# A Winograd convolution on one core: five edits to how it loads, warms up and stores

## The chip, the cores and the metric

The kernel runs on one core of a Trainium2 chip. Its time is in device microseconds (us); the lower the better. A set of runs is told by its median. The profile is of one execution, taken by the hardware profiler; its times are from the start of the span.

## The reference

A 3x3 convolution with padding 1 over 16 images of 64 channels and 64 x 64 pixels, to 128 output channels, all float32:

```python
def setup_inputs():
    batch, c_in, h, w, c_out = 16, 64, 64, 64, 128
    return {
        "x": np.random.randn(batch, c_in, h, w).astype(np.float32),
        "weight": np.random.randn(c_out, c_in, 3, 3).astype(np.float32) * 0.1,
    }

def reference(x, weight):
    x_pad = np.pad(x, ((0, 0), (0, 0), (1, 1), (1, 1)), mode='constant')
    ...
                        output[b, co] += weight[co, ci, kh, kw] * x_pad[b, ci, kh:kh+h, kw:kw+w]
    return output
```

The input is 16.8 MB and the output 33.6 MB.

## The kernel before, in words

Two images make a pair: 2 x 64 input channels fill the 128 partitions, so there are 8 pairs (`NP`), and each pair is worked on in two halves of 16 row pairs. `for n, (p, h) in enumerate(halves)` runs over the 16 halves. In the vertical direction the kernel computes two output rows at once (a Winograd scheme): from the input rows it forms sums (`ss`, L111), differences (`dd`, L118) and outer differences (`ee`, L124) in 16-bit floats, and a 16-bit copy of 17 rows (`xh`, L129). The first half's transforms are VectorE's (DVE), the second half's and all later ones are GpSimd's (POOL), which works two halves ahead; `xh` is ScalarE's (ACT), one half ahead. The seven weight combinations `Wt` (G0, G1, G2, G21, G01, HP, HM) are made once at the start: POOL casts the raw weights to `w16` (L82), TensorE (PE) transposes them by a multiplication with the identity (L98, in two runs, so that the result stands in partitions 0 to 63 and in 64 to 127), ACT and DVE combine them (L136 to L147).

`mms` (L167) issues the matmuls of a half, 54 of them, for the two images of the pair in turn (contraction over 64 partitions each). `copies` (L189, ACT) takes partial results out of PSUM, and DVE (L224, L226, L228) and ACT (L230) put together the output rows in `ots`, one tile of 128 output channels for each image. PSUM tiles with the tag "acc" share 8 buffers in turn; the first of them are used for the weights.

Inputs `xs` and outputs `ots` of 2.10 MB each share nine buffers of SBUF. Which one each uses is written out by hand: `X_HOME` for the loads, `O_HOME` for the two outputs of a pair. A tile's buffer is written again only when all that read it are done, a store's landing included.

Each engine works in the order in which the code names its instructions (`keep`). All transfers are issued by SyncE (SP), in one queue: the weights, the first pair in two pieces (rows 0 to 33, then 34 to 63), pairs 1 to 5; then, as results come, the stores, and the loads of pairs 6 and 7 behind the stores of pairs 2 and 3. Stores are of a whole image; only those of the last pair are cut by rows, 32 in each half. `spin` issues matmuls over a tile of zeros: 7 ahead of the weights' transposes and 9 behind them. Their result is not used.

Of the kernel before, what the change touches and what calls it, by code (L numbers as in the profile page):

```python
# [8 lines left out]
F32 = mybir.dt.float32  # L9
F16 = mybir.dt.float16  # L10
# [5 lines left out]
def kernel(  # L16
# [12 lines left out]
    nc = tc.nc  # L29
    B, CI, H, W = x.shape  # L30
    CO = weight.shape[0]
    assert H == 64 and W == 64 and CI == 64 and CO == 128 and B == 16
    NP = B // 2
    RB = 8

    keep = tc.keep_in_program_order
# [3 lines left out]
    const = ctx.enter_context(tc.tile_pool(name="const", bufs=1))  # L40
    psum = ctx.enter_context(tc.tile_pool(name="psum", bufs=8, space=bass.MemoryType.PSUM))
# [3 lines left out]
    upool = ctx.enter_context(tc.tile_pool(name="upool", bufs=8))  # L45

    X_HOME = [0, 1, 2, 3, 4, 7, 3, 4]
    O_HOME = [(6, 5), (8, 0), (1, 6), (2, 5), (8, 0), (1, 6), (7, 2), (5, 3)]

    def home(k, name):  # L50
        return slots.tile([128, H, W], F32, tag=f"s{k}", name=name)

    w_raw = const.tile([CO, CI * 9], F32)
# [3 lines left out]
    def load(p, cuts=((0, H),)):  # L57
        xs[p] = home(X_HOME[p], "xs")
        for lo, hi in cuts:
            keep(  # L60
                nc.sync.dma_start(
                    xs[p][:, lo:hi, :], x_rows[128 * p : 128 * p + 128, lo:hi, :]
                )
            )

    load(0, ((0, 34), (34, H)))
    for p in range(1, 6):
        load(p)

    zeros = const.tile([128, 512], F16)  # L70
    keep(nc.vector.memset(zeros, 0.0))  # L71
    warm = psum.tile([128, 512], F32, tag="acc", name="warm")

    def spin(n):
        for _ in range(n):
            keep(nc.tensor.matmul(warm, zeros[:, 0:128], zeros))  # L76

    spin(7)
    ident = const.tile([128, 128], F16)
    make_identity(nc, ident)  # L80
    w16 = const.tile([CO, CI * 9], F16)
    keep(nc.gpsimd.tensor_copy(w16, w_raw))  # L82

    G0, G1, G2, G21, G01, HP, HM = range(7)
    Wt = const.tile([128, 7, 3, CO], F16)
# [7 lines left out]
    for kh in (0, 2, 1):  # L93
        wp = psum.tile([128, 512], F32, tag="acc", name="wp")
        for k in range(3):
            t = 3 * kh + k
            for q in (0, 64):
                keep(nc.tensor.matmul(wp[q : q + 64, k * CO : k * CO + CO], w16[:, t::9], ident))  # L98
        wps[kh] = wp[:, 0 : 3 * CO]
    spin(9)  # L100


    F_BLK, G_BLK = (1, 2), (0, 3)
# [23 lines left out]
    def cast(p, h):  # L127
        t = cpool.tile([128, 17, W], F16, tag="xh", name="xh")
        keep(nc.scalar.copy(t, xs[p][:, C_ROW[h] : C_ROW[h] + 17, :]))  # L129
        return t  # L130

    def transforms(eng, p, h):
        return sums(eng, p, h), diffs(eng, p, h), outers(eng, p, h)
# [17 lines left out]
    def mms(tiles, terms, start, stop):  # L151
        n = 3 * len(terms)
        i = 0
        for wi, src, row in terms:
            for kw in (1, 0, 2):
                c_lo, c_hi = max(0, 1 - kw), min(W, W + 1 - kw)
                lo, hi = 0, RB
                at, step, rows = row
                while at + step * lo < 0:
                    lo += 1  # L160
                while at + step * (hi - 1) > rows - 1:
                    hi -= 1
                first, last = at + step * lo, at + step * (hi - 1)
                for b2 in range(2):
                    p0 = 64 * b2
                    keep(
                        nc.tensor.matmul(  # L167
                            tiles[b2][:, lo:hi, c_lo:c_hi],
                            Wt[p0 : p0 + 64, wi, kw, :],
                            src[  # L170
                                p0 : p0 + 64,
                                first : last + 1 : step,
                                c_lo + kw - 1 : c_hi + kw - 1,
                            ],
                            start=start and i == 0,
                            stop=stop and i == n - 1,
                            skip_group_check=not start,
                        )
                    )
                i += 1  # L180

    def acc():
        return [psum.tile([128, RB, W], F32, tag="acc", name="acc") for _ in range(2)]

    def copies(tiles):
        us = []
        for b2 in range(2):
            ut = upool.tile([128, RB, W], F32, tag="ut", name="ut")
            keep(nc.scalar.copy(ut, tiles[b2]))  # L189
            us.append(ut)  # L190
        return us

    halves = [(p, h) for p in range(NP) for h in range(2)]

    def store(eng, p, b2, ot, lo, hi):
        keep(eng.dma_start(out[2 * p + b2, :, lo:hi, :], ot[:, lo:hi, :]))  # L196

    for n, (p, h) in enumerate(halves):
        if n + 2 < len(halves):
            tr[halves[n + 2]] = transforms(nc.gpsimd, *halves[n + 2])  # L200
        if h == 0:
            ots = [home(k, "ot") for k in O_HOME[p]]
            ov = [t.rearrange("p (j i) c -> p j i c", i=2) for t in ots]
        ss, dd, ee = tr.pop((p, h))
        xc = xh.pop((p, h))
        jf, jg = RB * F_BLK[h], RB * G_BLK[h]
        sf, sg = jf - 16 * h, jg - 16 * h
        g_at = 2 * jg - C_ROW[h]

        pf1, pg1, pf2, pg2 = acc(), acc(), acc(), acc()  # L210
        mms(pf1, [(HP, ss, (sf, 1, 16))], True, True)
        ux = copies(pf1)
        mms(pg1, [(G1, ss, (sg, 1, 16))], True, True)
        ug = copies(pg1)
        mms(pf2, [(HM, dd, (0, 1, RB))], True, True)
        uy = copies(pf2)
        if n + 1 < len(halves):
            xh[halves[n + 1]] = cast(*halves[n + 1])
        mms(pg2, [(G01, xc, (g_at, 2, 17)), (G2, xc, (g_at + 2, 2, 17))], True, True)
        mms(pf1, [(G0, ee, (0, 2, 16))], False, True)  # L220
        mms(pg1, [(G21, xc, (g_at + 1, 2, 17)), (G0, xc, (g_at - 1, 2, 17))], False, True)
        mms(pf2, [(G2, ee, (1, 2, 16))], False, True)
        for b2 in range(2):
            keep(nc.vector.tensor_add(ov[b2][:, jg : jg + RB, 1, :], pg2[b2], ug[b2]))  # L224
        for b2 in range(2):
            keep(nc.vector.tensor_add(ov[b2][:, jf : jf + RB, 0, :], pf1[b2], uy[b2]))  # L226
        for b2 in range(2):
            keep(nc.vector.tensor_sub(ov[b2][:, jf : jf + RB, 1, :], ux[b2], pf2[b2]))  # L228
        for b2 in range(2):
            keep(nc.scalar.copy(ov[b2][:, jg : jg + RB, 0, :], pg1[b2]))  # L230
        if h == 1 or p == NP - 1:
            lo, hi = (0, H) if p < NP - 1 else (32 * h, 32 * h + 32)
            store(nc.sync, p, 0, ots[0], lo, hi)
            store(nc.sync, p, 1, ots[1], lo, hi)
            if p in (2, 3):
                load(p + 4)


# [28 lines left out]
```

## Time and profile before

| | |
|---|---|
| Median of 3 runs | 128.31 us (127.98 to 128.99) |
| The profiled execution | 127.76 us |
| Its span in the profile | 125.8 us |
| PE / PEld busy | 100.2 / 49.9 us |
| DVE / ACT / POOL busy | 67.3 / 84.8 / 90.5 us |
| The queue of all transfers | 50.63 MB, 95.8% of the span of 16 DMA engines |
| HBM read / written | 17.07 / 33.55 MB |
| Loads of 2.10 MB, from issue to landing | 20.3 us (median) |
| Stores of 2.10 MB, from issue to landing | 18.2 us (median) |

How to read it: PE is the matmuls, PEld the loading of their weights beside them. "L124" is a line of the kernel. The span is cut into 40 slices of equal length; a digit is the busy share of a slice in tenths. "A <- B" in a list of waits says that A waited and B ended the wait. The span does not hold all of the execution's time: 2.0 us lie around it.

### The profile page before, as it was taken

How to read it: one execution, taken by the hardware profiler on the slowest of the kernel's cores; microseconds unless marked ns; L12 is line 12 of the kernel's file. 1: busy time of each engine (PE TensorE's matmuls, PEld its weight loads, DVE VectorE, ACT ScalarE, POOL GpSimd, SP SyncE). 2: the span in 40 equal slices, each digit the busy share in tenths (PEclk: the TensorE clock that was granted, in tenths of full speed). 3: DMA queues.
4: the chain of work that ended last, by engine and by line, in shares of the span. 5: the costliest groups of instructions: out<-in, count | busy, mean ns of one | idle time of the engine just before them, and what ended most of it. 6: DMA issues, size and time to landing. Idle time of an engine off the chain costs nothing.

```text
span 125.8 us, 2404 instructions
## 1 busy us (share of the span) xinstructions
PE 100.2 (80%) x898; PEld 49.9 (40%) x898; DVE 67.3 (53%) x105; ACT 84.8 (67%) x149; POOL 90.5 (72%) x52
## 2 busy tenths in 40 slices
PE   6997899999993799999999999999999995000000
PEld 2443444444441355555555555555555552000000
DVE  0299849393820956749393947657493939000000
ACT  4269398979792679898979797898989783000000
POOL 2209999999999999999999999999999300000000
PEclk9999999999999999999999999999999999855555
DMA  5899999999999999999999999999999999999970
GB/s 144 351 438 438 427 433 433 422 422 417 360 425 427 427 425 443 427 417 420 433 433 433 422 433 417 433 433 435 422 427 427 422 453 412 433 412 425 422 313 18
DMA packets 4043, 50.78 MB, mean 404 GB/s; under 512 B 448, under 2 KB 448, under 8 KB 704
## 3 DMA queue, kind: packets, MB, share of 16 engines
q1 hardware_dynamic: 4032, 50.63, 95.8%
q8 instruction: 7, 0.11, 0.3%
q14 instruction: 4, 0.03, 0.1%
HBM read 17.07 MB, written 33.55 MB: 403 GB/s over the span
## 4 chain that ended last, share of the span: by engine, by line
PE 57%; DMA 19%; DVE 7%; DVEq 0%; ACT 0%; issue 0%; SPq 0%; ACTq 0%
PE acc L167 57%; DMA out_dram<-ot 15%; DMA xs<-in_x_dram 5%; DVE ee L124 2%; DVE ot L228 1%; DVE ot L226 1%; DVE ss L111 1%; DVE dd L118 0%; DVEq L262 0%; ACT ot L230 0%; DVE Wt L145 0%; DVE Wt L142 0%; DVE Wt L147 0%; SPq L54 0%; SPq L196 0%
## 5 line engine op out<-in xcount | busy, mean ns | idle before, releaser
L167 PEld LDWEIGHTS <-Wt 64*128 64x128 f16 x864 | 47.0, 94 | 50.3 <-issue 4.4
L189 ACT COPY ut<-acc 128x512 f32<-128x512 f32 x96 | 48.6, 612 | 4.4 <-PE acc L167 4.3
L167 PE MATMUL acc<-xh,Wt 64*128 64x504 f16 (+3 forms) x384 | 49.7, 370 | 0.0
L111 POOL TENSOR_TENSOR ss<-xs 128x1024 f16<-128x1024 f32 x15 | 35.6, 2373 | 5.3 <-DMA xs<-in_x_dram 5.3
L224 DVE TENSOR_TENSOR ot<-acc,ut 128x512 f32<-128x512 f32 x32 | 20.7, 686 | 33.2 <-ACT ut L189 19.6
L124 POOL TENSOR_TENSOR ee<-xs 128x1024 f16<-128x1024 f32 x15 | 35.6, 2372 | 0.0
L167 PE MATMUL acc<-ee,Wt 64*128 64x504 f16 (+1 forms) x192 | 30.3, 377 | 1.3 <-DVE ee L124 1.3
L167 PE MATMUL acc<-ss,Wt 64*128 64x504 f16 (+1 forms) x192 | 26.0, 377 | 2.9 <-DVE ot L224 2.6
L230 ACT COPY ot<-acc 128x512 f32<-128x512 f32 x32 | 17.3, 589 | 12.0 <-PE acc L167 10.1
L228 DVE TENSOR_TENSOR ot<-ut,acc 128x512 f32<-128x512 f32 x32 | 20.5, 683 | 0.6 <-PE acc L167 0.4
L226 DVE TENSOR_TENSOR ot<-acc,ut 128x512 f32<-128x512 f32 x32 | 20.4, 680 | 0.0
L118 POOL TENSOR_TENSOR dd<-xs 128x512 f16<-128x512 f32 x15 | 20.3, 1350 | 0.0
L129 ACT CAST xh<-xs 128x1088 f16<-128x1088 f32 x16 | 18.4, 1152 | 0.0
L167 PE MATMUL acc<-dd,Wt 64*128 64x504 f16 (+1 forms) x96 | 15.1, 377 | 0.0
L76 PE MATMUL warm<-zeros 128*128 128x512 f16 x16 | 5.8, 527 | 1.2 <-DVE zeros L71 1.2
L76 PEld LDWEIGHTS <-zeros 128*128 128x128 f16 x16 | 1.8, 124 | 3.9 <-issue 2.1
L138 DVE SCALAR_TENSOR_TENSOR th<-wp,g0h 128x384 f32<-128x384 f32 x1 | 0.6, 558 | 4.4 <-ACT g0h L136 4.4
L124 DVE TENSOR_TENSOR ee<-xs 128x1024 f16<-128x1024 f32 x1 | 2.8, 2833 | 0.0
L136 ACT ACTIVATE g0h<-wp 128x384 f32<-128x384 f32 x1 | 0.5, 492 | 2.9 <-PE wp L98 2.9
L82 POOL CAST w<-w_raw 128x576 f16<-128x576 f32 x1 | 0.7, 662 | 2.3 <-DMA w_raw<-in_weight_dram 2.3
L136 ACT ACT_TABLE_LOAD x1 | 1.3, 1283 | 0.7 <-PEq L251 0.7
L98 PEld LDWEIGHTS <-w 128*64 128x64 f16 x18 | 1.1, 210 | 0.9 <-POOL w L82 0.9
(17 smaller groups left out, 8.0 us busy)
## 6 DMA issues: line engine op xcount, KB each, us to landing
out_dram<-ot SPq DMA_DIRECT2D x14, 2048.0 KB, 18.2
xs<-in_x_dram SPq DMA_DIRECT2D x7, 2048.0 KB, 20.3
out_dram<-ot SPq DMA_DIRECT2D x4, 1024.0 KB, 17.5
xs<-in_x_dram SPq DMA_DIRECT2D x1, 1088.0 KB, 5.8
xs<-in_x_dram SPq DMA_DIRECT2D x1, 960.0 KB, 7.7
w_raw<-in_weight_dram SPq DMA_DIRECT2D x1, 288.0 KB, 2.8
```

The source lines that it names most:

```text
L76: keep(nc.tensor.matmul(warm, zeros[:, 0:128], zeros))
L111: keep(eng.tensor_add(t, v[:, j : j + 16, 0, :], v[:, j : j + 16, 1, :]))
L118: keep(eng.tensor_sub(t, v[:, j : j + RB, 1, :], v[:, j : j + RB, 0, :]))
L124: keep(eng.tensor_sub(t, xs[p][:, r - 1 : r + 15, :], xs[p][:, r + 1 : r + 17, :]))
L129: keep(nc.scalar.copy(t, xs[p][:, C_ROW[h] : C_ROW[h] + 17, :]))
L136: keep(nc.scalar.mul(g0h, wps[0], 0.5))
L167: nc.tensor.matmul(tiles[b2][:, lo:hi, c_lo:c_hi], Wt[p0 : p0 + 64, wi, kw, :], src[p0 : p0 + 64, first : last + 1 : step, c_lo + kw - 1 : ...
L189: keep(nc.scalar.copy(ut, tiles[b2]))
L224: keep(nc.vector.tensor_add(ov[b2][:, jg : jg + RB, 1, :], pg2[b2], ug[b2]))
L226: keep(nc.vector.tensor_add(ov[b2][:, jf : jf + RB, 0, :], pf1[b2], uy[b2]))
L228: keep(nc.vector.tensor_sub(ov[b2][:, jf : jf + RB, 1, :], ux[b2], pf2[b2]))
L230: keep(nc.scalar.copy(ov[b2][:, jg : jg + RB, 0, :], pg1[b2]))
```

## The change

- The first pair is loaded by one transfer of 64 rows.
- The matmuls over zeros (`zeros`, `warm`, `spin`) are gone.
- The raw weights are cast twice into one tile, by POOL and by ACT, and each of nine transposes gives both copies, where eighteen gave one each.
- Pair 5, the sixth load, is no longer issued at the start but behind the stores of pair 0. Pairs 6 and 7 stay behind the stores of pairs 2 and 3.
- The last pair is stored whole, after its second half.
- The second store of pair 1 and the stores of pairs 2, 3 and 4 are cut in two by output channels, that is, by partitions 0 to 63 and 64 to 127.

```diff
+    NEXT_LOAD = {0: 5, 2: 6, 3: 7}
...
-    load(0, ((0, 34), (34, H)))
-    for p in range(1, 6):
+    load(0)
+    for p in range(1, 5):
         load(p)
 
-    zeros = const.tile([128, 512], F16)
-    keep(nc.vector.memset(zeros, 0.0))
-    warm = psum.tile([128, 512], F32, tag="acc", name="warm")
-
-    def spin(n):
-        for _ in range(n):
-            keep(nc.tensor.matmul(warm, zeros[:, 0:128], zeros))
-
-    spin(7)
     ident = const.tile([128, 128], F16)
     make_identity(nc, ident)
-    w16 = const.tile([CO, CI * 9], F16)
-    keep(nc.gpsimd.tensor_copy(w16, w_raw))
+
+    w16 = const.tile([CO, 2, CI * 9], F16)
+    keep(nc.gpsimd.tensor_copy(w16[:, 0, :], w_raw))
+    keep(nc.scalar.copy(w16[:, 1, :], w_raw))
...
         for k in range(3):
-            t = 3 * kh + k
-            for q in (0, 64):
-                keep(nc.tensor.matmul(wp[q : q + 64, k * CO : k * CO + CO], w16[:, t::9], ident))
+            keep(nc.tensor.matmul(wp[:, k * CO : k * CO + CO], w16[:, :, 3 * kh + k :: 9], ident))
         wps[kh] = wp[:, 0 : 3 * CO]
-    spin(9)
...
-    def store(eng, p, b2, ot, lo, hi):
-        keep(eng.dma_start(out[2 * p + b2, :, lo:hi, :], ot[:, lo:hi, :]))
+    SPLIT = (2, 3, 4)
+
+    def store(p, b2, ot):
+        n = 64 if p in SPLIT or (p, b2) == (1, 1) else 128
+        for c in range(0, CO, n):
+            keep(nc.sync.dma_start(out[2 * p + b2, c : c + n, :, :], ot[c : c + n, :, :]))
...
-        if h == 1 or p == NP - 1:
-            lo, hi = (0, H) if p < NP - 1 else (32 * h, 32 * h + 32)
-            store(nc.sync, p, 0, ots[0], lo, hi)
-            store(nc.sync, p, 1, ots[1], lo, hi)
-            if p in (2, 3):
-                load(p + 4)
+        if h == 1:
+            store(p, 0, ots[0])
+            store(p, 1, ots[1])
+            if p in NEXT_LOAD:
+                load(NEXT_LOAD[p])
```

## The prediction

> **What bounds the kernel now.** I read the page's slices first, then its queue and chain parts, then the timeline of the start and of the one big hole, then windows. Two lines of the slices and the queue line say the most (40 slices of 3.145 us; busy tenths of the 16 DMA engines, and what they moved):
>
> ```profile
> DMA  5899999999999999999999999999999999999970
> GB/s 144 351 438 438 427 433 433 422 422 417 360 425 427 427 425 443 427 417 420 433 433 433 422 433 417 433 433 435 422 427 427 422 453 412 433 412 425 422 313 18
> ...
> q1 hardware_dynamic: 4032, 50.63, 95.8%
> ```
>
> The transfers never stop. 50.63 MB (8 loads of 2.10 MB, the weights, 33.55 MB of stores) must pass one queue at about 427 GB/s: 118.6 us, of a span of 125.8 us. One transfer of 2.10 MB is thus 4.9 us, one of 1.05 MB 2.46 us. The compute engines finish long before; SP's waits show by how much:
>
> ```profile
> SPq L262 <- DMA out_dram<-ot: 17.4, 1, 17.4
> ```
>
> L262 is the end of the program: the last 17.4 us are stores draining. So what counts is not how long PE works (57% of the chain that ended last is PE, because that chain runs back through the work which released the last store) but whether the DMA queue ever runs dry, and how fast one byte moves. The start, where it could run dry, from the timeline (start, duration, engine, line):
>
> ```profile
> 1.19 3.17 PE L76 MATMUL warm<-zeros 128*128 128x512 f16 x7 [1.19 <-DVE zeros L71]
> ...
> 6.97 1.23 DVE L111 TENSOR_TENSOR ss<-xs 128x1024 f16<-128x1024 f32 x1 [0.27 <-DMA xs<-in_x_dram]
> ...
> 8.58 0.68 DVE L118 TENSOR_TENSOR dd<-xs 128x512 f16<-128x512 f32 x1
> ...
> 9.51 2.36 POOL L111 TENSOR_TENSOR ss<-xs 128x1024 f16<-128x1024 f32 x1 [5.25 <-DMA xs<-in_x_dram]
> ...
> 10.12 2.83 DVE L124 TENSOR_TENSOR ee<-xs 128x1024 f16<-128x1024 f32 x1
> ...
> 11.82 2.26 POOL L118 TENSOR_TENSOR dd<-xs 128x512 f16<-128x512 f32 x1
> ...
> 15.53 1.46 PE L167 MATMUL acc<-ss,Wt 64*128 64x512 f16 x12
> ...
> 21.29 1.46 PE L167 MATMUL acc<-ss,Wt 64*128 64x512 f16 x12
> ...
> 22.25 12.68 SPq L196 DMA_DIRECT2D out_dram<-ot  x4
> ```
>
> DVE starts on the 34-row piece at 6.97; POOL gets the rest at 9.51. DVE and POOL hold each other up: DVE's ee (2.83) is twice its ss of the same size (1.23), since it ends only after POOL's ss; POOL's dd (2.26; later ones take 1.28) ends only after DVE's ee. A half costs PE 5.76 us (15.53 to 21.29), a pair 11.5. The first stores are issued at 22.25 and wait behind loads that are still running. Adding up the GB/s row, five loads and the weights (10.78 MB) are through at 27.7 us, the sixth at 33.
>
> **The change, part by part.**
>
> *First pair whole, no matmuls over zeros, weights twice.* One transfer in place of 34 + 30 rows saves at most 0.1 us of queue time. But DVE's first ss now waits for all 64 rows, about 9.3 (where POOL was released) in place of 6.97. Weights are no obstacle: ACT copies the second w (128x576, about 0.65 us between its 0.48 for 384 columns and 1.15 for 1088) beside POOL's 0.66; 9 transposes take no longer than 18 did (1.32). From 9.3 DVE and POOL want the same thing at once, so I string them up as they did before: DVE ss to 10.5, POOL ss to 12.8, DVE dd to 13.5, POOL dd to 14.7 (G01 and G21 pass meanwhile), DVE ee to 15.9, against 12.95 before. PE's first half then depends on its clock. Before, the 16 matmuls over zeros kept PE busy from 1.19; their weight loads stand 0.43 us apart up to 6.4 and 0.2 apart from 6.73 on, and the trace's clock record has the full rate from 6.63. Without them PE comes to its first ss matmuls at 10.55 at half rate, 12 in 2.6 us, dd at 13.95 (its PSUM bank waits for G01), and xh behind it. If the full rate comes at 16 to 17 (5.4 us after steady work began, as before), xh ends at 17.3 and the 24 matmuls left (2.5 us) at 19.9, not 15.53: +4.4 us. If it comes at 13.5, +2.9; if not before 20, +6.9. The first stores move from 22.25 to 26.7 (25.2 to 29.2).
>
> [...]
>
> *Sixth load behind the first stores.* This moves 4.9 us of queue work from ahead of the first stores to behind them, so total work is unchanged, but the cover shrinks: loads now end at 27.7, not 33. From issue to first byte is about 1 us (the first load is issued at 1.16 and the slices fill from there). Stores issued at 26.7 arrive at 27.7: idle 0. At 25.2 none, at 29.2 idle 2.5. I take +0.7, nearer to the early end because the central case is just covered. Later the queue stays ahead: stores of pair 0 and the sixth load run to 42.9, pair 1 is ready at 38.2; its stores run to 52.7, pair 2 is ready at 49.7; with the seventh load to 67.5, pair 3 at 61.2. The sixth load, landed by 43, is first read when POOL reaches pair 5, after 56 us. On SP nothing but stores stands behind it, and its issue (0.34 us) waits for nothing that is late.
>
> A stall also goes. Before, PE stopped at 38.5 to 42.7 since pair 2 writes into the buffer of pair 0's first store, which landed only at 40.64 behind six loads:
>
> ```profile
> 22.25 18.39 DMA out_dram<-ot
> ...
> 40.71 0.59 ACT ot L230
> ```
>
> Now that store lands near 34. The 4.2 us are a gain for PE that pays back the later start (pair 7 done at 107.2, before 106.0), and nothing for the end, since the queue is late next.
>
> *Last pair stored whole.* Four transfers of 1.05 MB become two of 2.10: -0.1 us. The upper rows wait for the second half, but at 107.2 the queue still has pair 6 to move (14 stores and 3 loads from 28.2 at 4.92 us each: 111.8), a cover of some 3.6 us after issue. Without cover it would cost up to 4.9.
>
> *Seven stores by channel halves* (pair 1's second, pairs 2, 3 and 4): 14 transfers from 64 partitions. The trace has none such. The nearest row is the last pair's 1.05 MB store, by row halves over 128 partitions: half the bytes, half the time, landings 2.46 us apart. By it the cost is 0. The issues add 7 x 0.34 us on SP, which waits 86.7 us for DVE anyway. The other bound: if half the partitions give half the rate, each half takes the 4.9 us of a whole, 14 x 2.46 = +34.4. The lower bound is 0: the queue already moves at its steady rate, and no row shows any transfer faster. I take 0, by the nearest row, and keep 34 for the range.
>
> [...]
>
> *Sum:* 125.8 span - 0.1 - 0.1 + 0.7 + 0 = 126.3. The profiled execution took 127.76 with its 2.0 us around the span, so 128.3; the median of the runs shown is 0.55 above it: **128.8 us**. Own range of this case 127.4 to 130.4.
>
> **Rivals.**
> *Half the lanes, half the rate.* From pair 1's second store to pair 4, 14 transfers run at half rate; decided by whether the DMA engines, all on the same 64 partitions, get in each other's way. For it: the steady rate is only ever seen with 128 partitions; nothing shows that 64 feed it. Against: loads and stores, of 8 and 16 KB a row, all move at that one rate, as if the DMA engines set it. The sixteen parts of one store complete over 2.5 us (38.14 to 40.64 in the trace's completions), a good transfer of 1.05 MB, so while some engines read upper partitions others still read lower ones. That gives part back, at most some 2 us of each store: +20 to +34, middle +27: 156 us.
> *The queue runs dry at the start.* PE stays at half rate past 20 us or POOL takes the shared turn first: stores at 29.5 to 30, idle 2.8 to 3.3: 131.2 us. For it: without the zeros PE is idle from 6 to 10.5. Against: five loads still give cover to 27.7.
> *Faster.* One stretch moves much less than its neighbours (columns: stretch, length, busy PE, PEld, DVE, ACT, POOL, clock, DMA share, GB/s):
>
> ```profile
> 28.00:31.00 3.00, 3.00 (x32) 1.37 (x29) 1.05 (x2) 3.00 (x7) 3.00 (x3) 1.00 1.03 426
> 31.00:34.00 3.00, 3.00 (x32) 1.37 (x28) 2.96 (x6) 2.34 (x4) 3.00 (x3) 1.00 0.95 322
> ```
>
> That is where the sixth load meets the first stores: 3 us at 322 in place of 427 lose 0.74. And the last two slices (313 and 18 GB/s) lose (114 + 409) / 427 x 3.145 = 3.9 us in which only some DMA engines still work. If another order avoids the dip, and the channel halves, which give each DMA engine other rows, even out a third of the tail: -0.2 - 0.7 - 1.3, 126.1 us. For it: both losses are there to be won. Against: nothing in the change aims at either, and the dip may move with the first stores.
>
> **How the numbers follow.** This kernel's measurement can tell about 1% (1.3 us) from no change. The forecast's case has a chance of 0.46: 0.04 of it faster by more, 0.28 within, 0.14 slower (above 129.6). Half rate has 0.30, the dry start 0.12, all slower. Faster has 0.12: 0.11 faster, 0.01 within. Sums: faster 0.15, same 0.29, slower 0.56. So the likeliest single case is no change, while most of the chance lies on the slow side. The range leaves out some 0.06 below 126.8 and the upper half of the half-rate case, 0.15, above 156.
>
> **What would show it.** In the slices after: first stores issued near 26.7 and no slice below 400 GB/s ahead of them; if they are issued past 28, the clock or POOL's turn is the cause, to be seen in DVE's ee end (15.9) and the length of the first half's matmuls. No PE hole at 38 to 42. Stores of channel halves landing 2.46 us apart and 427 GB/s from 45 to 100 us; if those slices fall toward 215 the half-rate case holds, and the forecast is wrong by its largest term. SP's last wait near 16 us, since pair 7 ends near 107; if it shrinks below 11, the last pair's whole stores have lost their cover.

## The result, and the profile after

The changed kernel takes 143.94 us (median of 6 runs, 137.42 to 147.94), the kernel before 127.94 us (6 runs, 127.73 to 128.99). By medians that is 12.5% slower. Single runs of the changed kernel differ by far more than those of before; its two quickest, 137.4 and 139.0 us, give a ratio of 1.079 (95% interval 1.070 to 1.088). The profile is of the slowest of the six, 147.94 us, with a span of 146.1.

The lines of the page that answer to those of before:

```profile
DMA  6999999999999999999999999999999999962000
GB/s 175 408 431 431 431 435 426 417 431 431 420 354 424 345 287 332 343 345 345 332 422 408 408 420 404 417 354 278 314 386 404 395 431 431 408 274 121 40 27 18
...
q1 hardware_dynamic: 3712, 50.63, 89.1%
```

A slice is now 3.65 us. The bytes are the same, and up to the thirteenth slice (47 us), with its one dip to 354, so is the rate. Then, when pair 1's second store comes up, the rate falls to 287 to 345 for seven slices, to 278 at 100 us, and in the last five slices from 274 down to 18, though by then every store has been issued. The busy digits show none of the first two losses: they stay at 9. Windows make that plain (the last two columns are the busy share of the DMA engines and GB/s):

```profile
38.00:48.00 10.00, 10.00 (x98) 5.09 (x94) 6.74 (x11) 8.75 (x16) 10.00 (x6) 1.00 1.01 398
48.00:58.00 10.00, 10.00 (x98) 5.09 (x94) 5.97 (x11) 9.12 (x16) 10.00 (x6) 1.00 1.00 313
...
118.00:128.00 10.00, 0.00 (x0) 0.00 (x0) 0.00 (x0) 0.00 (x0) 0.00 (x0) 0.50 0.99 423
128.00:138.00 10.00, 0.00 (x0) 0.00 (x0) 0.00 (x0) 0.00 (x0) 0.00 (x0) 0.50 0.34 147
138.00:146.00 8.00, 0.00 (x0) 0.00 (x0) 0.00 (x0) 0.00 (x0) 0.00 (x0) 0.50 0.05 23
```

From 48 to 58 us all 16 DMA engines are "busy" (1.00) and move 313 GB/s: by the trace's packet records the 16 KB packets begun in that stretch take 0.83 us in the mean, against 0.62 from 20 to 40 us, with 63 of 190 over 0.9. From 128 on only 34%, then 5% of them work: 0.05 of 16 is less than one engine. So there are two losses: slower packets, and a tail in which a few late DMA engines finish alone.

The start, against the times that I had strung up (start, duration, engine, line):

```profile
8.82 1.23 DVE L102 TENSOR_TENSOR ss<-xs 128x1024 f16<-128x1024 f32 x1 [2.07 <-DMA xs<-in_x_dram]
8.88 3.38 POOL L102 TENSOR_TENSOR ss<-xs 128x1024 f16<-128x1024 f32 x1 [4.53 <-DMA xs<-in_x_dram]
...
10.43 2.37 DVE L109 TENSOR_TENSOR dd<-xs 128x512 f16<-128x512 f32 x1
...
13.66 1.35 DVE L115 TENSOR_TENSOR ee<-xs 128x1024 f16<-128x1024 f32 x1
...
18.44 1.47 PE L158 MATMUL acc<-ss,Wt 64*128 64x512 f16 x12
...
25.18 0.93 SPq L191 DMA_DIRECT2D out_dram<-ot  x2
```

DVE and POOL hold each other up as foreseen (POOL's ss 3.38 for 2.36, DVE's dd 2.37 for 0.68), DVE's ee ends at 15.0 and the first stores are issued at 25.18, before the fifth load has landed (from 27.9 us on the first of the 16 DMA engines to 29.5 on the last, by the trace's completions). The queue does not run dry.

### The profile page after: what moved, and what is told of

Its sections match the earlier page's. It is cut to its first block, busy times and chain, and to the rows that moved or that the text cites. A ratio compares the mean times of both kernels' runs of the same rounds, so it can differ in the third digit from the quotient of the medians.

```text
span 146.1 us, 2360 instructions
## 1 busy us (share of the span) xinstructions
PE 99.0 (68%) x873; PEld 49.2 (34%) x873; DVE 67.1 (46%) x104; ACT 85.7 (59%) x150; POOL 92.0 (63%) x52
## 4 chain that ended last, share of the span: by engine, by line
PE 40%; DMA 25%; POOL 8%; issue 2%; DVE 1%; DVEq 0%; SPq 0%; POOLq 0%
PE acc L158 40%; DMA xs<-in_x_dram 25%; POOL ss L102 4%; POOL ee L115 3%; POOL dd L109 2%; DVE ss L102 1%; DVE ot L223 0%; DVEq L256 0%; SPq L55 0%; POOLq L102 0%; POOLq L109 0%
## 5 line engine op out<-in xcount | busy, mean ns | idle before, releaser
L158 PEld LDWEIGHTS <-Wt 64*128 64x128 f16 x864 | 48.3, 97 | 58.5 <-issue 14.4
L158 PE MATMUL acc<-xh,Wt 64*128 64x504 f16 (+3 forms) x384 | 47.4, 379 | 0.0
L102 POOL TENSOR_TENSOR ss<-xs 128x1024 f16<-128x1024 f32 x15 | 36.4, 2430 | 12.5 <-DMA xs<-in_x_dram 12.5
L115 POOL TENSOR_TENSOR ee<-xs 128x1024 f16<-128x1024 f32 x15 | 36.5, 2432 | 0.0
L158 PE MATMUL acc<-ee,Wt 64*128 64x504 f16 (+1 forms) x192 | 26.3, 377 | 0.0
L109 POOL TENSOR_TENSOR dd<-xs 128x512 f16<-128x512 f32 x15 | 19.5, 1301 | 0.0
L90 PE MATMUL wp<-ident,w 128*128 128x128 f16 x9 | 1.1, 312 | 4.5 <-POOL w L75 4.5
L90 PEld LDWEIGHTS <-w 128*128 128x128 f16 x9 | 0.9, 160 | 4.4 <-POOL w L75 4.4
L109 DVE TENSOR_TENSOR dd<-xs 128x512 f16<-128x512 f32 x1 | 2.4, 2370 | 0.0
L102 DVE TENSOR_TENSOR ss<-xs 128x1024 f16<-128x1024 f32 x1 | 1.2, 1226 | 2.1 <-DMA xs<-in_x_dram 2.1
```

The lines of the kernel that those rows point to most:

```text
L90: keep(nc.tensor.matmul(wp[:, k * CO : k * CO + CO], w16[:, :, 3 * kh + k :: 9], ident))
L102: keep(eng.tensor_add(t, v[:, j : j + 16, 0, :], v[:, j : j + 16, 1, :]))
L109: keep(eng.tensor_sub(t, v[:, j : j + RB, 1, :], v[:, j : j + RB, 0, :]))
L115: keep(eng.tensor_sub(t, xs[p][:, r - 1 : r + 15, :], xs[p][:, r + 1 : r + 17, :]))
L158: nc.tensor.matmul(tiles[b2][:, lo:hi, c_lo:c_hi], Wt[p0 : p0 + 64, wi, kw, :], src[p0 : p0 + 64, first : last + 1 : step, c_lo + kw - 1 : ...
```

## The experiments

In all of them times are medians in us, with the kernel before at 128.0 to 128.2 on the same chip. Theory A says that the transfers of 64 partitions cost; theory B that the start and the moved load do; rival C that it is the number of transfers.

**e1: whole stores, the five other edits of the list kept.**

```diff
-        n = 64 if p in SPLIT or (p, b2) == (1, 1) else 128
+        n = 128
```

> The changed kernel with all stores whole again; its four other edits stay. Theory A (half the lanes: the cost lies in the transfers of 64 partitions): 128 to 130 us, the forecast's own case, no slice under 400 GB/s from 10 to 110 us apart from a dip of under 1 us where the first stores begin. Theory B (the late first load, the cold start and the moved sixth load cost): still above 135 us.

Measured: 127.49 (127.15 to 129.29, 10 runs), ratio 0.995 (0.991 to 0.999). Theory B falls: the whole loss is in the channel halves. The page of e1:

```profile
DMA  5899999999999999999999999999999999999960
GB/s 167 355 449 444 423 418 433 412 407 439 433 439 415 350 415 433 423 423 441 423 423 423 423 433 433 428 418 431 423 428 428 433 423 428 428 439 428 439 298 31
```

One dip is left, 350 near 42 us, where the sixth load now ends; before, a slice of 360 stood at 31 to 35 us, where it ended then. The dip moved with that load.

**e2: the kernel before, with nothing but the cut stores.**

```diff
-        keep(eng.dma_start(out[2 * p + b2, :, lo:hi, :], ot[:, lo:hi, :]))
+        n = 64 if p in SPLIT or (p, b2) == (1, 1) else 128
+        for c in range(0, CO, n):
+            keep(eng.dma_start(out[2 * p + b2, c : c + n, lo:hi, :], ot[c : c + n, lo:hi, :]))
```

> The kernel before with nothing but the same seven stores cut by channel halves. Theory A: 136 to 150 us, as the changed kernel, with slices near 330 to 350 GB/s from pair 1's second store on, and a spread of single runs of several us. Theory B: 128 us, as before.

Measured: 141.85 (140.22 to 147.87). The cut alone makes the loss, and the wide spread of runs with it. The row of its profiled run (140.77 us, slices of 3.47 us) has both dips of the changed kernel, 293 to 345 and 274, and a shorter tail:

```profile
GB/s 145 374 444 434 444 406 439 439 411 359 427 415 432 434 340 293 321 342 345 335 330 439 415 415 396 389 434 382 274 278 354 420 444 434 408 427 425 269 99 14
```

**e3: the same stores cut by rows.**

```diff
-        for c in range(0, CO, n):
-            keep(nc.sync.dma_start(out[2 * p + b2, c : c + n, :, :], ot[c : c + n, :, :]))
+        n = H // 2 if p in SPLIT or (p, b2) == (1, 1) else H
+        for r in range(0, H, n):
+            keep(nc.sync.dma_start(out[2 * p + b2, :, r : r + n, :], ot[:, r : r + n, :]))
```

> The changed kernel with the same seven stores cut into the same number of transfers of the same bytes, but by rows, so that each transfer has all 128 partitions. Theory A: 128 to 130 us, as with whole stores. Rival C (twice as many transfers cost: more issues on SP, more waits for the eight completion semaphores in turn, smaller pieces): 136 to 148 us, as the changed kernel.

Measured: 128.30 (127.56 to 129.55), ratio 1.000 (0.997 to 1.003). As many transfers of the same size, and no loss beyond 0.8 us over e1: rival C falls too.

**e4: the transfers by themselves.**

```python
for i in range(0, 4): store(i, 0, 128)                         # whole
gate(src)
for i in range(4, 8): store(i, 0, 64); store(i, 64, 128)       # channel halves
gate(src)
for i in range(8, 12): store(i, 0, 128, 0, 32); store(i, 0, 128, 32, 64)   # row halves
gate(src)
for i in range(12, 16): store(i, 32, 96)
gate(src)
for i in range(12, 16): store(i, 0, 64)
gate(src)
for i in range(12, 16): store(i, 64, 128)
...   # two whole loads, then two loads by partition halves
```

(Each loop is put on one line here; `gate` makes what follows wait until all before it has landed.)

> Only transfers, no convolution: the output's values are not computed. Stretches, each begun after the one before has landed (so with 1 to 2 us of start and landing in each): four whole stores of 2.10 MB; four images by channel halves; four by row halves; four stores of partitions 32 to 95; four of 0 to 63; four of 64 to 127 (1.05 MB each); two whole loads; two loads by partition halves. Whole stores: 19.5 us and 2 of start. Theory A, with the lanes set by which partitions are named: channel halves 34 to 41 us, row halves 21.5, partitions 32 to 95 about 12, 0 to 63 and 64 to 127 about 20 each, whole loads 12, loads by halves 18 to 22. Theory A, with only the number of partitions mattering: partitions 32 to 95 take 20 too. Rival C: channel and row halves alike, 21.5 to 25, and the three stretches of 1.05 MB stores about 12 each.

Windows inside the stretches, in order: whole; channel halves (three); row halves; partitions 32 to 95; 0 to 63; 64 to 127. The last two columns again are busy share and GB/s:

```profile
6.00:26.00 20.00, 0.00 (x0) 0.00 (x0) 1.00 0.99 419
28.00:34.00 6.00, 0.00 (x0) 0.00 (x0) 1.00 0.90 202
...
40.00:46.00 6.00, 0.00 (x0) 0.00 (x0) 1.00 0.99 295
46.00:52.00 6.00, 0.00 (x0) 0.00 (x0) 1.00 0.99 333
...
62.00:78.00 16.00, 0.00 (x0) 0.00 (x0) 1.00 1.01 419
83.00:90.00 7.00, 0.00 (x0) 0.00 (x0) 1.00 0.99 419
94.00:112.00 18.00, 0.00 (x0) 0.00 (x0) 1.00 1.04 216
117.00:135.00 18.00, 0.00 (x0) 0.00 (x0) 1.00 0.99 204
```

This settles what is slow. Partitions 0 to 63 and 64 to 127 move at half the rate (216, 204), partitions 32 to 95, as many, at the full rate (419). In the trace's packet records a row of 16 KB takes 0.61 us in the whole stores and 1.27 us, just over twice that, in the two slow stretches. Why the two outer halves are slow and the middle is not, no run shows.

The channel halves in turn show something else: they start at 202 and rise to 333 GB/s. All eight took 33.6 us, not the 39 of a steady half rate. Meanwhile the 16 DMA engines, whose completions of one transfer lay 0.2 us apart at first, drifted 5 us apart. Hence theory D: in step, all engines read the low partitions, then all the high ones, and hold each other up (that two share one way is the theory's assumption, which no trace shows); out of step, some read low and some high. The packet records bear the difference out, as far as the packets of one DMA engine can be strung together by their ends and starts: from 36 to 44 us, where both occur, the median packet takes 1.20 us while at least 13 of the other 15 engines read the same half, and 0.61 us while fewer than 9 do. Loads by halves took about 5 us for each 1.05 MB too (two in 9.7 us, the next two in 9.2), as much as a whole load (4.9 in e5).

**e5: put them out of step on purpose.** Four images by channel halves, the same again behind a load of 8 partitions, and then whole loads.

```python
halves(0); gate(src); gate(few)
keep(nc.sync.dma_start(few, x_rows[0:8, :, :]))
halves(4)
...
for k in (0, 1, 2, 3, 4, 5, 6, 7, 5, 4): ...   # whole loads of pair k
```

> Only transfers again, no convolution: the output's values are not computed. First four images by channel halves as in e4 (33.6 us there, the transfers starting 4.3 us apart and ending 3 apart while the DMA engines' completions drift from 0.2 to 5 us). Then the same four images behind one load of 8 partitions (0.13 MB), which should hold up half of the DMA engines by about one 1.05 MB transfer's time. Theory D (two DMA engines in step share one way into 64 partitions; out of step, one reads low partitions while the other reads high ones, and nothing is lost): about 24 to 28 us for the second four images. Rival E (transfers of 64 partitions are slow at first for another reason and speed up with time or number): 33 to 36 us again. Then whole loads of pairs 0 to 7, then 5 and 4 again, to see whether the dip that stood at the end of the sixth load in every profile belongs to that part of the input: if so, the loads of pair 5 take over 5.5 us, all others 4.9; if it belongs to what runs beside it in the full kernel, all take 4.9.

Measured: first group 33.4 us, second 33.6, from the windows of the second:

```profile
41.00:47.00 6.00, 0.00 (x0) 0.00 (x0) 1.00 1.01 232
...
59.00:65.00 6.00, 0.00 (x0) 0.00 (x0) 1.00 0.96 336
...
90.00:110.00 20.00, 0.00 (x0) 0.00 (x0) 1.00 1.01 432
```

A miss: the time is what rival E said. The test did not do what it was built for, since the small load held its 8 DMA engines only from 39.6 to 41.0 us while the halves began at 40.2: under 1 us out of step, not 2.4. What it does show is that the rise is not a matter of time or number since the program's start: all engines wait for each other between the groups, and the second group begins slow again. A speeding-up that starts anew after each such wait is not excluded by this run; the packets of e4 that are quick or slow in the same stretch (0.61 and 1.20 us) speak against it. Whether engines share a way, and which with which, stays open. The loads of pair 5 took 4.9 us like all others (their landings stand 4.9 us apart throughout), so the dip at the end of the sixth load does not belong to that part of the input; what it does belong to also stays open.

**e6, e7: one cut store, and all sixteen.**

```diff
-        n = 64 if p in SPLIT or (p, b2) == (1, 1) else 128
+        n = 64 if (p, b2) == (1, 1) else 128     # e6
+        n = 64                                   # e7
```

> The changed kernel with one store only, pair 1's second, cut by channel halves. Theory D: DMA engines come to it nearly in step (1 us apart), so it costs almost the full 4.9 us less twice that spread, 2.5 to 4 us over the 127.5 of whole stores: 130 to 131.5 us. A linear share of the seven (16.5 / 7 = 2.35 us): 129.8 us. If whole stores behind it let the DMA engines catch up: 127.5 to 128.

> The changed kernel with all sixteen stores cut by channel halves. Linear in the number of cut stores: 127.5 + 16 x 2.35 = 165 us. Theory D: the DMA engines drift apart and the later cuts cost less, 145 to 158 us, with the GB/s row low at first (near 330) and rising; if they stayed in step throughout, 127.5 + 16 x 4.9 = 206 us.

Measured: 134.62 with one cut store (131.40 to 136.31), 136.37 with sixteen (135.97 to 137.62). Both expectations were off: by medians one costs 7 us, more than the 4.9 that two half-rate transfers can lose by themselves (the quickest of its four runs costs 4.2), and sixteen cost less than seven, though by the quickest runs only by 1.5 us (135.97 and 137.42). The row of e7:

```profile
GB/s 165 394 433 428 433 428 433 418 307 287 277 268 319 311 392 423 423 421 423 404 409 365 394 418 418 387 409 409 438 414 443 414 448 409 443 423 428 375 214 34
```

It is slow for six slices (268 to 319) and then runs mostly above 400, with every store cut. Over those six the spread of completions grows to 8 us; it is 9 at the end. This is as theory D has it: out of step, channel halves run almost at the full rate, though D's own figure for the whole kernel, 145 to 158 us, was too high. In e6 one cut store drives the spread from 3.3 to 7.6 us, and it is still 6.7 at the end. Its windows show the cut store, the whole transfers behind it, and the end:

```profile
51.00:57.00 6.00, 6.00 (x61) 3.07 (x57) 4.10 (x8) 5.34 (x10) 6.00 (x4) 1.00 1.03 284
...
62.00:125.00 63.00, 43.24 (x402) 21.96 (x398) 30.01 (x48) 37.14 (x66) 37.78 (x20) 0.88 1.00 418
125.00:132.00 7.00, 0.00 (x0) 0.00 (x0) 0.00 (x0) 0.00 (x0) 0.00 (x0) 0.50 0.19 82
```

Whole transfers go on at nearly the full rate (418 GB/s) but do not bring the engines back together.

**e8: cut in three, 32 to 95 first.**

```diff
+        cuts = ((32, 96), (0, 32), (96, 128)) if p in SPLIT or (p, b2) == (1, 1) else ((0, 128),)
+        for c, e in cuts:
+            keep(nc.sync.dma_start(out[2 * p + b2, c:e, :, :], ot[c:e, :, :]))
```

> The changed kernel with the seven stores cut in three by channels, 32 to 95, 0 to 31 and 96 to 127: the same bytes, more and smaller transfers. If what counts is which partitions are named (e4: 32 to 95 moved at full rate), half of the bytes go at full rate and the cost halves: 134 to 138 us. If every cut by channels costs, 144 us and more.

Measured: 143.62 (136.78 to 144.62), as much as in the changed kernel, by the quickest run too (137.42 there). The loss did not halve although 32 to 95 alone moves at full rate (419 GB/s in e4): what that transfer costs between others is not decided by its own rate. The pieces 0 to 31 and 96 to 127 were not measured by themselves.

**e9, e10, e11: where the cut stores stand.** From e6 to e8 theory F: a cut store drives the DMA engines apart, and each change back to whole transfers costs again, since late engines then share with early ones that are already in the next transfer.

```diff
+        n = 64 if 2 * p + b2 >= 9 else 128       # e9: the last seven
+        n = 64 if (p, b2) == (7, 1) else 128     # e10: the very last
+        n = 64 if b2 == 0 else 128               # e11: the first of each pair
```

> The changed kernel with seven stores cut by channel halves again, but the last seven (pair 4's second to pair 7), so that no whole transfer comes behind them. Theory F (a cut store drives the DMA engines out of step, once, by up to 9 us as in e7; and every change back to whole transfers while they are out of step costs more, since late ones must share with early ones that are already in the next transfer): 133 to 137 us, like all sixteen cut (136.4) and less than seven in the middle (143.9). If the number of cut stores decides: 144 us as in the changed kernel.

> The changed kernel with only the very last store cut by channel halves. Nothing is queued behind it, so the cost is its own: at most 4.9 us if the DMA engines come to it in step, less what their spread of 3.6 us gives back: 129 to 131 us, less than e6's 134.6, where twelve whole stores and two loads follow the one cut store. If one cut store costs the same wherever it stands: 134 us.

> The changed kernel with the first store of each pair cut and the second whole: eight cut stores, eight changes back to whole ones. Theory F: more than with all sixteen cut, 145 to 165 us. If only the drift counts, and it comes to an end when the DMA engines are far enough apart: 133 to 137 us, no more than the 136.4 of all sixteen.

Measured: e9 134.50 (133.88 to 137.17), e10 129.81 (129.22 to 130.08), e11 162.0 (154.3 to 166.7). All three as theory F said, and against the number of cut stores. The loss over e1, with "changes back" the times that a whole transfer, store or load, follows a cut store:

| | cut stores | changes back | by medians, us | by the quickest runs, us |
|---|---|---|---|---|
| e10 | 1 | 0 | 2.3 | 2.1 |
| e9 | 7 | 0 | 7.0 | 6.7 |
| e6 | 1 | 1 | 7.1 | 4.2 |
| e7 | 16 | 3, each to one load | 8.9 | 8.8 |
| changed kernel | 7 | 3 | 16.5 | 10.3 |
| e11 | 8 | 8 | 34.5 | 27.2 |

At the same number of cut stores the kernel with changes back costs more (one: e6 over e10; seven: the changed kernel over e9), and eight with eight changes cost far more than sixteen with three. That changes back cost is shown by these times; how much one costs is not: e7's three add little. That late engines share with early ones is the theory's inference from the times and from the packets below; no run shows it. The open dip at the sixth load also plays in: in e9's profile (137.17 us, its slowest run) it is deeper, 324 and 293 GB/s, long before any cut store. The row of e11 (slices of 4.0 us) does not come back to the steady rate for long and ends in the longest tail:

```profile
GB/s 180 425 425 446 433 421 429 278 221 388 378 292 405 360 368 317 303 364 348 409 384 386 356 401 393 360 352 311 335 278 356 307 303 307 294 192 65 29 41 33
```

From the trace's packet and completion records of the profiled runs (3072 packets of 16 KB each, which take 0.61 us in the median in the changed kernel):

| | cut stores | packets over 0.9 us | over 1.4 us | last transfer complete on the first DMA engine / median of the 16 / on the last, us |
|---|---|---|---|---|
| e1 | 0 | 41 | 4 | 121.0 / 122.5 / 124.6 |
| e7 | 16 | 207 | 23 | 124.9 / 130.5 / 133.8 |
| changed kernel | 7 | 254 | 50 | 125.3 / 131.4 / 145.2 |
| e11 | 8 | 506 | 124 | 135.0 / 143.4 / 159.3 |

In these four the order of the times is the order of the packets that take longer; among all the profiled kernels with as many such packets it is nearly so (e9 has 183 at 137.2 us, e7 207 at 136.7; e8 259 at 144.0, the changed kernel 254 at 147.9). A packet over 1.4 us is longer than twice 0.61, which is all that two sharers would give by theory D. In the changed kernel the first engine is done at 125.3, 4 us later than in e1; the program ends with the last, 20 us later, 13.9 of them behind the median and the final 8.3 with no other engine at work (the last but one is done at 136.9). The last completion fell 3.6 us behind the next at the load of pair 7 and 7.5 us in pair 4's first store. That made the load late, as a line of the chain that ended last shows:

```profile
67.15 28.42 DMA xs<-in_x_dram
```

PE stood still for it, and pair 7 was ready at 113 in place of 107 us; with stores queued to 145, that cost nothing more. In e2, with the same seven cut stores and a profiled run of 140.77 us, the median engine is done at 131.9 us and the last at 137.8: the 7 us between these two profiled runs lie with the last engine alone. That the wide spread of times comes from this fits, but of each kernel only one run was profiled.

**e12: whole stores again, more rounds.**

> The kernel of e1 once more, in more rounds, to see whether the four other edits gain: by e1's ratio (0.995, 0.991 to 0.999) 127.4 to 127.6 us beside 128.0; if e1's difference was chance, a ratio within 0.002 of 1.

Measured: 127.55 (127.22 to 128.45, 12 runs) against 128.24, ratio 0.995 (0.992 to 0.998). This version is quicker than the changed kernel and 0.5% under the kernel before. The two sets of runs agree and their intervals lie clear of 1, but 0.5% is less than the 1% that the prediction took as the least this measurement can tell.

## Why the prediction was right and wrong

The time lies inside the range (126.8 to 156.0) and on the side that had most of the chance. That it does is owed to the width of the range, and in part to luck: the number, 128.8, is 15 us too low and fits another kernel, the changed one without channel halves (127.5) or with row halves (128.3), and the rival that stretched the range put its middle at 156, by a sum that does not hold either.

- *"I take 0, by the nearest row."* This is the step that failed: the term put at 0 came to 16.5 us by medians, 10.3 by the quickest runs (against e1). The row was the store of 1.05 MB by row halves, and e3 shows that for cuts by rows it was right. But it has all 128 partitions, and the steady rate of the page had never been seen with fewer. I took "that one rate, as if the DMA engines set it" for a reason; e4 has the same DMA engines, equally busy (1.04), at 216. The rival of half the rate had the right kind of loss, and I left it at 0.30, behind a row of another shape; for two halves in turn, half the rate held only while the DMA engines were in step (e4: 202 GB/s at first, 333 later).
- *Half the lanes, half the rate: 156.* Right in kind, too high by 12. The way back that I named, DMA engines out of step, is real (e4: 202 to 333 GB/s while the completions drift 5 us apart; e7: mostly above 400 with 8 to 9), and stronger than the 2 us a store allowed for it: 16.5 us were lost by medians (143.94 less e1's 127.49) where 14 x 2.46 = 34.4 was the bound. But the shape was wrong: I priced each cut store alone and added seven times. The loss is not a sum over cut stores. As far as the runs show, it comes from driving the engines apart (e6: from 3.3 to 7.6 us), from the changes between kinds of transfer while they are apart (seven cut stores: 7.0 us in e9 without changes back, 16.5 with three), and from waiting for the last engine (13.9 us behind the median in the profile after).
- *The start, +0.7.* Too pessimistic. The first pair landed at 8.8, not 9.3, and the full clock came at about 15 us: the weight loads of PE stand 0.43 us apart up to 14.95 and 0.2 from 15.28 on, 5.2 us after its matmuls of `ss` began at 10.11, and the trace's clock record has the full rate from 15.18. First stores at 25.18 (25.09 in e1) for 26.7: the queue stayed covered by 1.5 us, and the term is 0.
- *Sixth load, last pair whole: the stall goes, the end does not move.* Right. PE has no hole at 38 to 42 us in the changed kernel, and SP's last wait for landings, in the list of its waits in e1, is 17.3 us, where 17.4 stood before and 16 was forecast:

```profile
SPq L256 <- DMA out_dram<-ot: 17.3, 1, 17.3
```

- *The sum without channel halves.* 128.3 on the profile's own scale against e1's profiled 127.31: 1.0 us too high, 0.7 of it the start. Why the five other edits together gain 0.5% was not taken apart (the list of the change has six edits, not the five of the title).
- *Faster, by losing the dip.* The dip moved instead of going, as the rival's own objection had it, but by about 9 us, with the sixth load, and not by 3 us, with the first stores.

## What to carry to other kernels

A queue that is always busy can still move at half its rate (e4: 216 GB/s at a busy share of 1.04, whole stores 419 at 0.99): read GB/s beside the busy share, and take a steady rate as proven only for the shape of transfer that showed it. As far as e1, e3 and e8 show (127.5, 128.3 and 143.6 us), cut a transfer by rows, not by partitions, and keep all 128 partitions in each piece. And price a slow transfer in a full queue by what it does to those behind it: in a queue that was never empty, DMA engines that had lost step did not find it again (e6: 6.7 us apart at the end), and the program ended with the last of them (the changed kernel: 145.2 us, the median engine 131.4).

## What was unexpected in the hardware

- Partitions 0 to 63 or 64 to 127 alone: 216 and 204 GB/s; 32 to 95, as many: 419; all 128: 419 (e4).
- Low and high halves in turn begin at 202 GB/s and rise to 333 within 24 us, as the DMA engines drift 5 us apart (e4).
- One cut store among whole ones, with 14 transfers behind it, costs 7 us by medians (4.2 by the quickest runs); one at the very end 2.3 (2.1); all sixteen 9 (8.8); every other one 34 (27).
